# Two-model kernel on one core: the spread of the joined weights of dilated attention issued later, and stick-breaking blocks placed on both halves of the array

## The chip, the cores and the metric

The kernel runs on one core of a Trainium2 chip. The metric is the time of one execution in microseconds of device time; lower is better. Matrix products run on TensorE (PE), loads of its weights are listed apart (PEld), and the other engines are VectorE (DVE), ScalarE (ACT), GpSimd (POOL, which also issues some transfers) and SyncE (SP, which issues the others). PE's sums go to banks of PSUM, everything else lies in SBUF with 128 partitions.

## The reference, cut to what matters

The program computes two models one after the other. The first (a mixer with a recurrent and a state-space branch, and a mixture of experts) is not touched. The second has two layers over 512 tokens of width 1024. Each layer normalises, projects once, runs three attentions over that projection, gates and merges them, and ends in a feed-forward part:

```
h = _rms_norm(x, attn_norm[l])
proj = h @ w_in[l]
...
o_a = _dilated_mixture(aq, ak, a_v.reshape(grp)).reshape(B, S, DSA_OUT)
...
o_c = _stick_breaking_attention(c_q.reshape(sb), c_k.reshape(sb), c_v.reshape(sb)).reshape(B, S, SB_OUT)
gates = jax.nn.sigmoid(gate.reshape(B, S, N_BRANCH, D_MODEL))
```

Stick breaking has 8 heads of width 64. For a block of 128 queries:

```
z = jnp.einsum('bqhd,bkhd->bhqk', qi, k, preferred_element_type=jnp.float32) * scale
strict = kpos[None, :] < qpos[:, None]
log_beta = jax.nn.log_sigmoid(z)
log_one_minus = jnp.where(strict, jax.nn.log_sigmoid(-z), 0.0)
after = lax.cumsum(log_one_minus, axis=3, reverse=True) - log_one_minus
weights = jnp.exp(jnp.where(strict, log_beta + after, -jnp.inf))
return jnp.einsum('bhqk,bkhd->bqhd', weights.astype(v.dtype), v)
```

Dilated attention has 4 heads in each of 3 groups (dilations 1, 4, 16); each group gives an output and the logarithm of its softmax sum per token and head, and the groups are joined by a softmax over those logarithms:

```
wts = jax.nn.softmax(jnp.stack(lses, axis=0), axis=0)
o = jnp.sum(wts[..., None] * jnp.stack(outs, axis=0).astype(jnp.float32), axis=0)
```

## The kernel before

Everything is built in float32. A large product is made of three products of rounded halves (`mm3`: lines 202, 205 and 206), and one 128-row tile of the gates takes 8 times 3 such products of 512 columns. These tiles depend on nothing in the attentions, so the kernel uses them as dense filler: `GATES = (9, 3, 2, 10)` says how many go beside each stage. A small attention product in plain float32 shows as two records (two passes) in the trace.

Two or more generators are woven by `merge`: each yields numbers, its clock advances by that number over the weight it was given, and the generator with the least clock goes next. `mark`, `paced`, `pin` and `after` tie a product to the one issued before it, so that the order of the woven generators stays the order of issue on PE; a scheduler orders the rest by data.

The **stick-breaking stage** of a layer weaves `sb_heads` with 9 gate tiles and half of the query preparation of another attention (`mla_half`). A pass of `sb_heads` issues the logits of head h (`sb_logits`: four diagonal blocks, L385, and three rectangles, L390, of k times q into the three PSUM tiles `z`), then finishes head h-1 (`sb_out`: masks and suffix sums by matrix products, L419 and after, three exponentials into `wt`, and the product with v, L439 and after, which the trace lists partly under L419). Head h uses the 64 partitions from 64*(h%2), so its logits fill 64 of the array's 128 rows; the product with v fills 64 of its 128 columns. The result goes by a DVE copy to `gev` and by a transfer to `od` in memory.

The **dilated stage** weaves `dsa_att` (weight 29.2) with the last 10 gate tiles (240 dense products) and with `branches`, which fetches the other attentions' results. `dsa_att` has 8 units, 4 query blocks for each of two pairs of heads: `logits` (L719 to L725), `softmax` on DVE and ACT, `pv` (transposes L754, products L765). After a pair's fourth unit `both(pr)` transposes the collected maxima and sums (L776), works out the joined weights `T`, two rows of 512 tokens (ACT L779, L781, L782, L785; DVE L780, L783, L784, L786, L787, reciprocal L788, L789), and spreads them over the 128 partitions by two products with the constant `sel` (L793, two rows deep), which L795 and L796 multiply into the outputs. Then `merge2` starts, with its own weights to convert (L183 on ACT, L184 on DVE).

Of the kernel before, what the change touches and what calls it, by code (L numbers as in the profile page):

```python
# [9 lines left out]
F32 = mybir.dt.float32  # L10
# [7 lines left out]
P = 128  # L18
D = 1024
S = 512  # L20
# [216 lines left out]
class Block2(Ctx):  # L237
# [130 lines left out]
    def sb_heads(self, p, pp, qT, kT, v, spill):  # L368
        st = {}
        for h in range(9):  # L370
            if h < 8:
                yield from self.sb_logits(p, pp, h, qT, kT, st)
            if h:
                yield from self.sb_out(p, pp, h - 1, v, st, spill)

    def sb_logits(self, p, pp, h, qT, kT, st):
# [7 lines left out]
        for b in range(4):  # L384
            i = nc.tensor.matmul(at(b * P, (b + 1) * P), k[:, diag(b)], q[:, diag(b)], start=(b == 0), stop=True,  # L385
                                 skip_group_check=True)
        self.mark(i)
        yield 1
        for b in (0, 2, 1):
            i = nc.tensor.matmul(at(*off[b]), k[:, diag(b)], q[:, (b + 1) * P:], start=(b != 2), stop=True,  # L390
                                 skip_group_check=True)
        self.mark(i)
        yield 2
        e = p.tile([P, W], F32, name="e", bufs=2)
# [17 lines left out]
    def sb_out(self, p, pp, h, v, st, spill):  # L412
# [4 lines left out]
        r = slice(64 * (h % 2), 64 * (h % 2) + 64)  # L417
# [21 lines left out]
        nc.tensor.matmul(ob[r, :P], vh[:, 0], wt[:, diag(0)], start=True, stop=False, skip_group_check=True)  # L439
        for b in range(4):  # L440
            if b:
                i = add(ob[r, diag(b)], vh[:, b], wt[:, diag(b)], b == 3)
            if b < 3:
                i = add(ob[r, (b + 1) * P:], vh[:, b], wt[:, slice(*off[b])])
            if b == 1:
                self.mark(i)
                yield 2
        self.mark(i)
        yield 1
        spill(h // 2, ob, r)  # L450
# [251 lines left out]
    def dsa_att(self, p, pp, oa):  # L702
# [69 lines left out]
        def both(pr):  # L772
# [17 lines left out]
            yield 0.5  # L790
            for o in range(2):
                R = pp.tile([P, 512], F32, name=f"s{o}", bufs=2)
                i = nc.tensor.matmul(R, self.k["sel"][:2], T[:, o], start=True, stop=True)  # L793
                self.mark(i)
                nc.vector.tensor_mul((oa[:, pr], oAB[pr][:, 1])[o], oAB[pr][:, o], R)  # L795
            nc.gpsimd.tensor_add(oa[:, pr], oa[:, pr], oAB[pr][:, 1])  # L796
            yield 1.7
# [3 lines left out]
        yield 1.3  # L801
        for n, u in enumerate(units):
# [5 lines left out]
            yield from pv(*u, es, w0)  # L808
            if u[1] == NT - 1:
                yield from both(u[0])  # L810
# [4 lines left out]
    def attn2(self, l, x, hh, hl):  # L815
# [5 lines left out]
        with ExitStack() as es0:  # L821
# [4 lines left out]
            def spill(i, ps, r=slice(0, P)):  # L826
                s = stage.tile([P, S], F32, name="gev", bufs=3)
                nc.vector.tensor_copy(s[r], ps[r])
                nc.gpsimd.dma_start(od[i, r], s[r])

# [17 lines left out]
            with self.pool(f"sb{l}") as p, self.pool(f"sbp{l}", psum=True) as pp:  # L848
# [8 lines left out]
                merge([(self.sb_heads(p, pp, qT, kT, v, spill), 8 * 11.5), (*fill(gates(g0)), -self.KICK2),  # L857
# [1784 lines left out]
```

## Time and profile before

| | |
|---|---|
| median of 3 runs | 4501.78 us (4495.5 to 4502.18) |
| profiled execution | 4502.9 us, span 4501.1 us |
| PE busy | 4108.9 us, 91% of the span |
| DVE, ACT, POOL busy | 2274.7 (51%), 1580.0 (35%), 981.2 us (22%) |
| the first layer's stick-breaking stage | 2471 to about 2630 us |
| the first layer's dilated stage | 2857 to about 2978 us |
| the second layer's | 3519 to about 3678 us, 3902 to about 4023 us |

The span is from the first to the last recorded event; the rest of the profiled execution's time, 1.8 us, lies around it. The granted clock of PE is given as a share of full speed: 1.00 is 2.4 GHz, 0.50 is 1.2 GHz. A busy engine is not one at its peak, and idle time of an engine that nobody waits for costs nothing; what counts is what PE waits for in the two stages.

### The profile page before, as it was taken

What the parts mean: (1) busy time and instruction counts of PE and PEld (TensorE: products, weight loads), DVE (VectorE), ACT (ScalarE), POOL (GpSimd) and SP (SyncE); (2) the same over time, 40 slices, a digit from 0 to 9 for tenths busy, and PEclk for the clock granted to TensorE, in tenths of its full rate; (3) what the DMA queues carried; (4) which work ended last, traced back from release to release, by engine and by line L of the source; (5) the groups of instructions that cost most, each with busy time, mean ns of one, the idle gap of its engine ahead of it and who ended that gap; (6) DMA issues with size and microseconds to landing.
All of it is one profiled execution on the core that took longest, in us unless ns stands there. A gap on an engine that the chain in (4) does not pass through costs nothing. (4 is left out here: it accounts for less than half of the span.)

```text
span 4501.1 us, 70132 instructions
## 1 busy us (share of the span) xinstructions
PE 4108.9 (91%) x28191; PEld 3030.7 (67%) x28191; DVE 2274.7 (51%) x4106; ACT 1580.0 (35%) x3184; POOL 981.2 (22%) x1272
## 2 busy tenths in 40 slices
PE   7899888798898888799998999989999999989998
PEld 5777665576665556444436778768888777858887
DVE  4666766656859865411113255454343244555332
ACT  3333332233346553200003554433233464433331
POOL 1333432334535542200001121130001021211000
PEclk9999999898999999899999999999999999989999
DMA  4222224322342336599993222243332222324332
GB/s 164 68 54 68 66 52 136 82 56 70 110 138 92 110 104 199 214 377 393 394 400 121 62 64 87 78 140 87 98 100 85 73 62 80 94 88 123 96 97 75
DMA packets 535698, 569.04 MB, mean 126 GB/s; under 512 B 126256, under 2 KB 426804, under 8 KB 534348
## 3 DMA queue, kind: packets, MB, share of 16 engines
q1 hardware_dynamic: 400940, 463.04, 30.7%
q0 software_dynamic: 21216, 71.42, 4.8%
q10 hardware_dynamic: 113216, 30.09, 3.2%
q8 instruction: 222, 3.64, 0.3%
q14 instruction: 104, 0.85, 0.1%
HBM read 508.40 MB, written 56.05 MB: 125 GB/s over the span
## 5 line engine op out<-in xcount | busy, mean ns | idle before, releaser
L202 PE MATMUL d<-hh,wh 128*128 128x512 f32 (+1 forms) x1952 | 861.3, 442 | 3.0 <-ACT wh L183 2.0
L205 PE MATMUL d<-hl,wh 128*128 128x512 f32 (+1 forms) x1952 | 782.9, 401 | 14.2 <-DVE hl L184 8.9
L206 PE MATMUL d<-hh,wl 128*128 128x512 f32 (+1 forms) x1952 | 781.1, 400 | 3.7 <-DVE wl L184 3.5
L183 ACT CAST wh<-wr 128x1024 fp32r<-128x1024 f32 (+2 forms) x509 | 433.4, 855 | 925.5 <-PE d L205 427.4
L184 DVE TENSOR_TENSOR wl<-wr,wh 128x1024 fp32r<-128x1024 f32 (+1 forms) x378 | 433.9, 1152 | 627.4 <-ACT wh L183 621.7
L202 PEld LDWEIGHTS d<-hh,wh 128*128 128x128 f32 x1952 | 378.4, 194 | 113.7 <-issue 46.7
L205 PEld LDWEIGHTS d<-hl,wh 128*128 128x128 f32 x1952 | 379.9, 195 | 91.3 <-issue 20.7
L206 PEld LDWEIGHTS d<-hh,wl 128*128 128x128 f32 x1952 | 377.4, 193 | 94.8 <-DVE wl L184 7.5
L184 POOL TENSOR_TENSOR wl<-wr,wh 128x512 fp32r<-128x512 f32 (+1 forms) x131 | 186.7, 1428 | 146.1 <-ACT wh L183 144.9
L202 PE MATMUL d<-wh,hh 128*128 128x256 f32 x704 | 205.4, 292 | 4.4 <-ACT wh L183 3.8
L202 PE MATMUL m<-wh,gh 128*128 128x512 f32 x512 | 200.3, 392 | 7.8 <-ACT wh L183 7.8
L205 PE MATMUL d<-wl,hh 128*128 128x256 f32 x704 | 202.9, 288 | 3.0 <-DVE wl L184 1.7
L206 PE MATMUL d<-wh,hl 128*128 128x256 f32 x704 | 202.0, 287 | 0.0
L205 PE MATMUL m<-wl,gh 128*128 128x512 f32 x512 | 200.3, 391 | 0.0
L206 PE MATMUL m<-wh,gl 128*128 128x512 f32 x512 | 200.0, 391 | 0.0
L202 PEld LDWEIGHTS d<-wh,hh 128*128 128x128 f32 x704 | 136.9, 195 | 6.4 <-ACT wh L183 4.2
L2498 PE MATMUL pa<-ew,XE 128*64 128x512 f32 x496 | 140.7, 602 | 0.0
L1681 POOL TENSOR_SCALAR Sl<-Sall,lam 128x64 f32<-128x64 f32 x176 | 96.1, 559 | 199.7 <-DVE Sall L1693 198.7
L205 PEld LDWEIGHTS d<-wl,hh 128*128 128x128 f32 x704 | 136.8, 194 | 3.9 <-DVE wl L184 2.1
L206 PEld LDWEIGHTS d<-wh,hl 128*128 128x128 f32 x704 | 136.7, 194 | 0.1
L2498 PE MATMUL pb<-ew,XE 128*64 128x512 f32 x504 | 127.9, 597 | 6.2 <-DMA ew<-in_exp_w_dram 6.2
L2498 PE MATMUL py<-ew,ec 128*64 128x512 f32 x512 | 130.5, 598 | 2.3 <-DMA ew<-in_exp_w_dram 2.3
(745 smaller groups left out, 8221.7 us busy)
## 6 DMA issues: line engine op xcount, KB each, us to landing
ew<-in_exp_w_dram SPq DMA_DIRECT2D x189, 1024.0 KB
wr<-in_w_ff_dram SPq DMA_DIRECT2D x128, 512.0 KB
wr<-in_w_in_dram SPq DMA_DIRECT2D x116, 512.0 KB
wr<-in_w_in_dram SPq DMA_DIRECT2D x167, 256.0 KB
wr<-in_ada_w_dram SPq DMA_DIRECT2D x64, 256.0 KB
sg<-gev POOLq DMA_DIRECT2D x48, 256.0 KB, 2.6
sgt<-sg POOLq DMA_DIRECT2D x48, 256.0 KB, 3.2
su<-u POOLq DMA_DIRECT2D x24, 384.0 KB, 3.1
```

The source lines that it names most:

```text
L183: i = self.high(hi, src)
L184: j = self.low.tensor_sub(lo, src, hi.bitcast(F32))
L202: i = nc.tensor.matmul(out, lh, rh, start=start, stop=False)
L205: nc.tensor.matmul(out, lh, rl, start=False, stop=False)
L206: self.latest = nc.tensor.matmul(out, ll, rh, start=False, stop=stop)
L1681: nc.gpsimd.tensor_scalar(Sl[:, d], S[:, d, n], lam[:, d, c:c + 1], None, op0=OP.mult)
L2498: nc.tensor.matmul(ps[c][64 * j:64 * j + 64], lhs(k + i, j), w_, start=(k + i == 0), stop=(k + i == KC - 1))
```

## The change

In the stick-breaking stage, `other(i)` copies the q and k of head pair i into `qk`, with the two groups of 64 partitions exchanged, by four transfers issued on POOL (16 in a layer). `sb_logits` takes the diagonal blocks and the rectangle `off[1]` from the head's own 64 partitions, and the rectangles `off[0]` and `off[2]` from the exchanged copy, in another order and with other yields. The product with v is cut into nine parts that alternate between output partitions 0 to 63 and 64 to 127, and write 256 columns instead of 512; `spill_sb` copies 128x256 instead of 64x512 and stores it with two transfers instead of one. `e` has one buffer instead of two.

In the dilated stage, `both` ends when `T` is computed. Its spread is a function `join`, called for the first pair after the next unit's `pv`, and for the second pair after a further yield of 9; its products are pinned behind the latest dense product. The stage's weight rises from 29.2 to 39, by which fewer dense products fall to each yield before that.

```diff
@@ -366,14 +366,25 @@
     SBO = {0: (512, 896), 2: (896, 1024), 1: (1024, 1280)}
 
     def sb_heads(self, p, pp, qT, kT, v, spill):
-        st = {}
+        st, swap = {}, []
+
+        def other(i):
+
+            x = p.tile([P, 2, S], F32, name="qk", bufs=2)
+            for j, src in enumerate((qT, kT)):
+                self.nc.gpsimd.dma_start(x[:64, j], src[64:, i])
+                self.nc.gpsimd.dma_start(x[64:, j], src[:64, i])
+            swap.append(x)
+        other(0)
         for h in range(9):
+            if h % 2 == 0 and h < 6:
+                other(h // 2 + 1)
             if h < 8:
-                yield from self.sb_logits(p, pp, h, qT, kT, st)
+                yield from self.sb_logits(p, pp, h, qT, kT, swap[h // 2], st)
             if h:
                 yield from self.sb_out(p, pp, h - 1, v, st, spill)
 
-    def sb_logits(self, p, pp, h, qT, kT, st):
+    def sb_logits(self, p, pp, h, qT, kT, qk, st):
         nc = self.nc
         off, W = self.SBO, self.SBW
         diag = lambda b: slice(b * P, (b + 1) * P)
@@ -381,17 +392,21 @@
         q, k = qT[r, h // 2], kT[r, h // 2]
         z = [pp.tile([P, 512], F32, name="z", bufs=6) for _ in range(3)]
         at = lambda a, b: z[a // 512][:, a % 512:a % 512 + b - a]
-        for b in range(4):
-            i = nc.tensor.matmul(at(b * P, (b + 1) * P), k[:, diag(b)], q[:, diag(b)], start=(b == 0), stop=True,
-                                 skip_group_check=True)
+        ro = slice(64 - 64 * (h % 2), 128 - 64 * (h % 2))
+        qo, ko = qk[ro, 0], qk[ro, 1]
+
+        mm = lambda a, b, k, q, start: nc.tensor.matmul(at(a, b), k, q, start=start, stop=True, skip_group_check=True)
+        mm(0, P, k[:, diag(0)], q[:, diag(0)], True)
+        mm(*off[0], ko[:, diag(0)], qo[:, P:], True)
+        for b in (1, 2, 3):
+            i = mm(b * P, (b + 1) * P, k[:, diag(b)], q[:, diag(b)], False)
+        i = mm(*off[2], ko[:, diag(2)], qo[:, 3 * P:], False)
+        self.mark(i)
+        yield 2
+        i = mm(*off[1], k[:, diag(1)], q[:, 2 * P:], True)
         self.mark(i)
         yield 1
-        for b in (0, 2, 1):
-            i = nc.tensor.matmul(at(*off[b]), k[:, diag(b)], q[:, (b + 1) * P:], start=(b != 2), stop=True,
-                                 skip_group_check=True)
-        self.mark(i)
-        yield 2
-        e = p.tile([P, W], F32, name="e", bufs=2)
+        e = p.tile([P, W], F32, name="e")
         pieces = ((0, 512), (512, 1024), (1024, 1280))
         for a, b in pieces:
             nc.scalar.activation(e[:, a:b], at(a, b), AF.Abs)
@@ -414,7 +429,6 @@
         off, W = self.SBO, self.SBW
         diag = lambda b: slice(b * P, (b + 1) * P)
         z, sp, ac = st.pop(h)
-        r = slice(64 * (h % 2), 64 * (h % 2) + 64)
 
         add = lambda o, a, b, stop=False: nc.tensor.matmul(o, a, b, start=False, stop=stop, skip_group_check=True)
         wt = p.tile([P, W], F32, name="wt", bufs=1)
@@ -436,18 +450,19 @@
         yield 1.5
         ob = z[0]
         vh = v[:, :, h * 64:(h + 1) * 64]
-        nc.tensor.matmul(ob[r, :P], vh[:, 0], wt[:, diag(0)], start=True, stop=False, skip_group_check=True)
-        for b in range(4):
-            if b:
-                i = add(ob[r, diag(b)], vh[:, b], wt[:, diag(b)], b == 3)
-            if b < 3:
-                i = add(ob[r, (b + 1) * P:], vh[:, b], wt[:, slice(*off[b])])
-            if b == 1:
+
+        U, D_ = slice(0, 64), slice(64, 128)
+        parts = [(U, 0, 0, 0), (D_, 0, 1, P), (U, P, 3, 3 * P), (D_, P, 2, 2 * P), (U, P, 0, 6 * P), (D_, 0, 0, 4 * P),
+                 (U, P, 2, 7 * P), (U, P, 1, 9 * P), (D_, P, 1, 8 * P)]
+        for n, (x, o, b, c) in enumerate(parts):
+            m = 2 * P if c == 4 * P else P
+            i = nc.tensor.matmul(ob[x, o:o + m], vh[:, b], wt[:, c:c + m], start=(n < 2), stop=True, skip_group_check=True)
+            if n == 3:
                 self.mark(i)
                 yield 2
         self.mark(i)
         yield 1
-        spill(h // 2, ob, r)
+        spill(h, ob)
 
 
     def attend(self, p, pp, units, logits, scale):
@@ -787,18 +802,21 @@
             nc.vector.tensor_add(T[:, 2], T[:, 2], T[:, 3])
             nc.vector.reciprocal(T[:, 2], T[:, 2])
             nc.vector.tensor_mul(T[:, :2], T[:, :2], T[:, 2:3].to_broadcast([2, 2, S]))
-            yield 0.5
+            return T
+
+        def join(pr, T):
             for o in range(2):
                 R = pp.tile([P, 512], F32, name=f"s{o}", bufs=2)
                 i = nc.tensor.matmul(R, self.k["sel"][:2], T[:, o], start=True, stop=True)
+                self.pin(i)
                 self.mark(i)
                 nc.vector.tensor_mul((oa[:, pr], oAB[pr][:, 1])[o], oAB[pr][:, o], R)
             nc.gpsimd.tensor_add(oa[:, pr], oa[:, pr], oAB[pr][:, 1])
-            yield 1.7
 
         units = list(product(range(2), range(NT)))
         nxt = logits(*units[0])
         yield 1.3
+        T = None
         for n, u in enumerate(units):
             w0 = nxt[1]
             es = softmax(*u, *nxt)
@@ -806,8 +824,16 @@
                 nxt = logits(*units[n + 1])
                 yield 1.3
             yield from pv(*u, es, w0)
+            if T is not None:
+                join(u[0] - 1, T)
+                T = None
+                yield 1.7
             if u[1] == NT - 1:
-                yield from both(u[0])
+                T = both(u[0])
+                yield 0.5
+        yield 9
+        join(1, T)
+        yield 1.7
 
 
     GATES = (9, 3, 2, 10)
@@ -827,6 +853,14 @@
                 s = stage.tile([P, S], F32, name="gev", bufs=3)
                 nc.vector.tensor_copy(s[r], ps[r])
                 nc.gpsimd.dma_start(od[i, r], s[r])
+
+            def spill_sb(h, ps):
+                s = stage.tile([P, S], F32, name="gev", bufs=3)[:, :2 * P]
+                nc.vector.tensor_copy(s, ps[:, :2 * P])
+                to = od[h // 2, 64 * (h % 2):64 * (h % 2) + 64].rearrange("p (q t) -> p q t", t=P)
+                v = s.rearrange("p (q t) -> p q t", t=P)
+                nc.gpsimd.dma_start(to[:, ::3], v[:64])
+                nc.gpsimd.dma_start(to[:, 1:3], v[64:])
 
             def gev(i, ps):
                 g = stage.tile([P, S], F32, name="gev", bufs=3)
@@ -854,7 +888,7 @@
                 run(self.tr_gen(w, C2["ck"], 512, hh, hl, KC, lambda i, ps: nc.scalar.copy(kT[:, i], ps)))
                 self.mla_prep1(l, pm)
                 run(self.nat_gen(w, C2["cv"], 512, hh, hl, KC, lambda t, c, m, ps: nc.scalar.copy(v[:, t, c:c + m], ps)))
-                merge([(self.sb_heads(p, pp, qT, kT, v, spill), 8 * 11.5), (*fill(gates(g0)), -self.KICK2),
+                merge([(self.sb_heads(p, pp, qT, kT, v, spill_sb), 8 * 11.5), (*fill(gates(g0)), -self.KICK2),
                        (self.mla_half(l, pm, 0), 18, 0.5)])
                 self.last = None
             pv = es.enter_context(self.pool(f"dsa{l}"))
@@ -876,7 +910,7 @@
                     self.dsa_pad = fill(gates(g2))[0]
                     run(self.dsa_qk(l, pq, px, pp, w, hh, hl))
                 with self.pool(f"dsb{l}") as p:
-                    merge([(self.dsa_att(p, pp, oa), 29.2),
+                    merge([(self.dsa_att(p, pp, oa), 39),
                            (*fill(gates(g3)), -self.KICK2), (self.branches(po, od, sp), 8)])
                     self.last = None
             es.close()
```

The order of issue on PE shows the second join of a layer. `T` are the joined weights, `s0` and `s1` the PSUM tiles that receive the spread, the rows L202, L205 and L206 are dense gate products. Before:

```order
L776 MATMUL t_26182<-ident_65,st_25434 98x128 x4
L202 MATMUL d_26144<-hh_21374,wh2_26140 128x512
L205 MATMUL d_26144<-hl_21375,wh2_26140 128x512
L206 MATMUL d_26144<-hh_21374,wl2_26141 128x512
L793 MATMUL s0_26202<-T_26187,sel_19207 128x512
L793 MATMUL s1_26205<-T_26187,sel_19207 128x512
L202 MATMUL d_26144<-hh_21374,wh2_26140 128x512
```

Of the change, with the first and the last of the dense products between:

```order
L791 MATMUL t_26141<-ident_65,st_25478 98x128 x4
L202 MATMUL d_26134<-hh_21374,wh0_26130 128x512
L205 MATMUL d_26134<-hl_21375,wh0_26130 128x512
...
L205 MATMUL d_26223<-hl_21375,wh2_26219 128x512
L206 MATMUL d_26223<-hh_21374,wl2_26220 128x512
L810 MATMUL s0_26246<-T_26146,sel_19207 128x512
L810 MATMUL s1_26249<-T_26146,sel_19207 128x512
```

Between the transposes and the spread there stood 3 dense products, and now 60. On DVE, the steps of the same `T` (L795 to L804) now have steps of other work between them; `wl` are the low halves of the weights of the stage that follows:

```order
L799 TENSOR_TENSOR T<-t,T 2x512
L801 TENSOR_TENSOR T<-T 2x1024
L802 TENSOR_TENSOR T<-T 2x512
L184 TENSOR_TENSOR wl_26287<-wr_26284,wh_26286 128x1024
L803 RECIPROCAL T<-T 2x512
L184 TENSOR_TENSOR wl_26293<-wr_26290,wh_26292 128x1024
L804 TENSOR_TENSOR T<-T 2x1024
```

Before, no other work stood between the steps of that `T`. The first join on PE, of the change (`pr` are softmax numerators, `pt` their transposes):

```order
L769 MATMUL t_25882<-ident_65,pr1_25837 128x128 x3
...
L780 MATMUL t_25891<-pt1_25886,v2_23243 64x128
L202 MATMUL d_25859<-hh_21374,wh0_25855 128x512
L205 MATMUL d_25859<-hl_21375,wh0_25855 128x512
L206 MATMUL d_25859<-hh_21374,wl0_25856 128x512
L769 MATMUL t_25969<-ident_65,pr0_25935 128x128 x4
L769 MATMUL t_25976<-ident_65,pr1_25941 128x128 x4
L810 MATMUL s0_25903<-T_25811,sel_19207 128x512
L810 MATMUL s1_25906<-T_25811,sel_19207 128x512
```

Before, the first spread came right behind the six products L765 of the unit that follows the pair; now 3 dense products and the 8 transposes of the unit after that stand ahead of it too. The logits of a head, on PE, before (`z` are the three logit tiles):

```order
L385 MATMUL z_22726<-qT_21771,kT_21772 128x128 x4
L202 MATMUL d_22719<-hh_21374,wh2_22715 128x512
L205 MATMUL d_22719<-hl_21375,wh2_22715 128x512
L206 MATMUL d_22719<-hh_21374,wl2_22716 128x512
L390 MATMUL z_22727<-qT_21771,kT_21772 128x384
L390 MATMUL z_22727<-qT_21771,kT_21772 128x128
L390 MATMUL z_22728<-qT_21771,kT_21772 128x256
```

and of the change:

```order
L398 MATMUL z_22758<-qT_21771,kT_21772 128x128
L398 MATMUL z_22759<-qk_22458 128x384
L398 MATMUL z_22758<-qT_21771,kT_21772 128x128 x3
L398 MATMUL z_22759<-qk_22458 128x128
...
L398 MATMUL z_22760<-qT_21771,kT_21772 128x256
```

The rectangles of 384 and 128 columns now stand among the diagonal blocks and read `qk`; six dense products stand ahead of the last rectangle.

## Rows read from the trace of the kernel before

**Rows 1.** Windows: length, busy us of PE, PEld, DVE, ACT, POOL, granted clock, DMA share, GB/s.

```profile
2471.00:2630.00 159.00, 158.37 (x820) 115.84 (x819) 56.22 (x78) 95.61 (x137) 33.41 (x51) 1.00 0.22 64
2857.00:2973.00 116.00, 95.34 (x536) 67.47 (x535) 49.41 (x79) 42.96 (x106) 6.15 (x10) 0.88 0.21 64
```

**Rows 2.** Waits of PE, dilated stage, first layer: total us, times, longest.

```profile
PE s L793 <- DVE T L789: 17.3, 2, 11.2
```

**Rows 3.** Timeline of PE, first join: start, us, what, count, idle before it.

```profile
2899.20 0.60 PE L776 MATMUL t<-ident,st 128*98 128x128 f32 x4
...
2914.10 3.78 PE L793 MATMUL s<-T,sel 2*128 2x512 f32 x4 [6.09 <-DVE T L789]
```

**Rows 4.** Timeline of PE, second join.

```profile
2956.73 0.49 PE L776 MATMUL t<-ident,st 128*98 128x128 f32 x3
...
2969.12 3.78 PE L793 MATMUL s<-T,sel 2*128 2x512 f32 x4 [11.20 <-DVE T L789]
```

**Rows 5.** Windows around the two joins, and their stretches at the lower clock.

```profile
2900.81:2923.10 22.29, 12.83 (x36) 6.98 (x35) 11.58 (x13) 6.15 (x15) 1.81 (x2) 0.63 0.11 36
2957.52:2978.11 20.59, 9.39 (x18) 5.31 (x17) 11.51 (x12) 5.71 (x8) 3.38 (x5) 0.59 0.08 26
2906.50:2923.57 17.07, 10.98 (x28) 6.25 (x28) 7.95 (x7) 1.13 (x2) 1.27 (x1) 0.50 0.00 0
2961.11:2978.18 17.07, 9.06 (x17) 5.37 (x18) 9.83 (x10) 3.30 (x5) 3.38 (x5) 0.50 0.10 31
```

**Rows 6.** Timeline of PE, stick breaking, one head's small products and their ends.

```profile
2530.38 0.43 PE L439 MATMUL z<-wt,v 128*64 128x128 f32 x2
...
2532.04 0.50 PE L202 MATMUL d<-hh,wh 128*128 128x512 f32 x1
...
2532.93 0.87 PE L419 MATMUL z<-wt,v 128*64 128x128 f32 x6
2533.73 0.50 PE L202 MATMUL d<-hh,wh 128*128 128x512 f32 x1
...
2534.62 1.16 PE L385 MATMUL z<-qT,kT 64*128 64x128 f32 x8
2535.70 0.50 PE L202 MATMUL d<-hh,wh 128*128 128x512 f32 x1
...
2536.60 1.56 PE L390 MATMUL z<-qT,kT 64*128 64x384 f32 x6
2538.09 0.50 PE L202 MATMUL d<-hh,wh 128*128 128x512 f32 x1
```

**Rows 7.** Timeline of PE, dilated stage: logits and products with v of one unit.

```profile
2870.91 0.70 PE L721 MATMUL s<-kT,qT 64*128 64x256 f32 x4
...
2871.99 0.51 PE L202 MATMUL d<-hh,wh 128*128 128x512 f32 x1
...
2877.22 1.20 PE L765 MATMUL t<-pt,v 128*64 128x128 f32 x16
```

**Rows 8.** Timeline of POOL and ACT ahead of the stick-breaking stage.

```profile
2475.88 1.00 POOL L601 COPY kn<-kr 128x128 f32<-128x128 f32 x4 [44.33 <-DVE qlTl L197]
...
2455.59 0.58 ACT L854 COPY kT<-d 128x512 f32<-128x512 f32 x1
```

**Rows 9.** Transfers by line, whole run: count, KB each, median us to landing.

```profile
od<-gev POOLq DMA_DIRECT2D x16, 128.0 KB, 2.3
```

**Rows 10.** Timeline of PE, dilated stage: dense products after one unit's logits.

```profile
2881.46 0.50 PE L202 MATMUL d<-hh,wh 128*128 128x512 f32 x1
...
2884.35 0.60 PE L754 MATMUL t<-ident,pr 128*128 128x128 f32 x4
```

**Rows 11.** Groups of DVE instructions, dilated stage: count, busy us, mean ns, idle before.

```profile
L184 DVE TENSOR_TENSOR wl<-wr,wh 128x1024 fp32r<-128x1024 f32 x9 | 11.0, 1222 | 5.4 <-ACT wh L183 5.4
```

**Rows 12.** Timelines of DVE and ACT: first and last step of one unit's softmax.

```profile
2881.56 1.29 DVE L738 TENSOR_REDUCE st<-s 128x2 f32<-128x512 f32 x2 [2.42 <-PE s L725]
...
2887.10 0.48 ACT L744 ACTIVATE pr<-s,sm 128x256 f32<-128x256 f32 x1
```

## Prediction, made before the changed kernel was timed

> **What bounds the kernel now.** I read the windows of the two stages first. In the stick-breaking stage PE is busy 158.4 of 159.0 us at full clock [rows 1]: nothing is waited for, and what counts is how long PE's own products take. In the dilated stage it is busy 95.3 of 116 us at a mean clock of 0.88 [rows 1], so there is idle time and slow time. The waits name the cause: the spread `sel` waits for `T` twice, 17.3 us in total and 11.2 at the longest [rows 2]. The timeline shows both places [rows 3, 4]: PE runs out of work that stands ahead of the spread, and sits idle 6.1 us before the first and 11.2 before the second. The windows around the two show that the harm outlasts the idling: from inside the first, 17.07 us run at clock 0.50 (1.2 GHz), and likewise at the second, and the last of those lie behind the spread [rows 5].
>
> What the two joins cost is window length less what the same products take at full clock. The prices: 12 dense products with their entry fill 2.89 us between logits and transposes [rows 10], of which about 0.11 is the change of array shape, so 0.232 each; a pass of 128 columns takes about 0.107 (14 such block passes in 1.66 us against 6 in 0.80 [rows 6]), so a 512-column pass 0.43. First join: 13 dense 3.0, 6 transposes 0.65, 12 passes of the product with v on both halves 0.65 plus entry 0.25, 4 passes of the spread 1.7, shape changes 0.2: 6.5 of 22.3 us [rows 5], 15.8 lost. Second: 13 dense 3.0, spread 1.7, changes 0.2: 4.9 of 20.6 [rows 5], 15.7 lost. The second layer has the same two waits of the same length, so 63 us are lost at four joins. No more than this can be won in the dilated stage.
>
> **The change part by part.**
>
> *The second join.* 60 dense products instead of 3 stand between the transposes and the spread: 13.9 us, with the transposes 14.4 us of work. The chain of `T` took 12.4 us from transposes to spread (2956.73 to 2969.12 [rows 4]). It gets longer: two subtractions `wl` of the next stage now stand between its steps on DVE, 1.22 us each [rows 11], so about 14.8 us, and PE waits some 0.5 us. That is too short for me to expect a fall of the clock. Saved: about 15 of 15.7 us; 13 if `T` comes 2.5 us late, 15.5 if the subtractions fit in gaps in which DVE waits for ACT. What is late next is L813 and with it `merge2`; the oa halves were waiting there before too, and the gate products of that tile run behind the spread as before.
>
> *The first join.* The chain took 14.9 us here (2899.20 to 2914.10 [rows 3]), longer because the softmax of the next units stands between its steps; I take 15.2, since now the reductions of one more unit do. By the order of issue, ahead of the spread now stand 21 dense products (4.9 us), the logits of a unit (1.6, of which 1.08 are small products [rows 7]), 14 transposes (1.4 us with 0.1 for changes of shape), 12 passes of products with v (0.9) and some 0.4 us of other changes of shape: 9.2 us. So PE still waits about 6 us, as it did before (6.09), only in one place instead of three, and the clock falls afterwards as before; I put 2.3 us on that, between nothing and 4 us (the spread took 3.78 us instead of 1.7 [rows 3], and the dense products behind it ran at half clock until 2923.57 [rows 5]). Lost 8.3 instead of 15.8: saved 7.5, between 2 (chain longer by 3 us, full cost of the clock) and 11 (the chain as before, no fall).
>
> *The dense products that pay for it* are the same 240. Before the spread of pair 1 the stage has about 57 fewer, so each unit has less between its logits and its transposes. Softmax of a unit takes from 2881.56 to 2887.58, 6.0 us, with other work between its steps [rows 12]. Its cover was 12.4 us (logits of one unit end at 2871.99 [rows 7], the transposes of that unit start at 2884.35 [rows 10]). By the order of issue a middle unit keeps 27 dense products (6.3), transposes (0.9), products with v (1.1) and the next logits (1.6): 9.9 us. 6.0 is hidden with nearly 4 to spare: cost 0. If that cover is gone, see the slower rival.
>
> *Stick breaking.* A head's logits took 1.08 and 1.49 us, its product with v 1.66 and 0.80 [rows 6]: 5.03. Do two halves of the array work at once? In the dilated stage they do, in this same kernel: the logits there, 8 block passes on each half, took 1.08 us (2870.91 to 2871.99 [rows 7]), as long as 8 on one half alone (2534.62 to 2535.70 [rows 6]), and 16 passes with v took 1.20 us [rows 7], where one half would take 1.9. So now: logits first part, 8 block passes a half, 1.13; the rectangle alone, 4 passes, 0.66 with entry; product with v, 4 and 6 passes a half, 0.69 and 0.91 with an offset of one pass between halves. Sum 3.39 us; 1.64 saved a head, 26 us for 16 heads. I take 25, because the first two and the last head's products are woven otherwise. The stage is bound by PE, so all of it should show.
>
> How strictly products follow each other is open: in the rows cited, neighbours on the two halves are equally long; here a 384-column rectangle stands among 128-column blocks. The Trainium skill (TensorE: Matmul & The Clock Gate, Part 3, The mechanism) says that products start and end in program order. By that the blocks behind the rectangle wait for its end, and the saving would be smaller; the rival below prices it.
>
> The 16 exchange transfers per layer stand on POOL's queue, which is idle for 44 us up to 2475.88 [rows 8], and the first pair's k is ready at 2456.2 [rows 8], 15 us before the first logits. Like transfers landed in 2.3 us [rows 9]. Later pairs are asked for a head or two ahead, some 15 us. Cost 0; without that cover, about 3 us once a layer. The smaller DVE copy and the second store cost POOL 0.55 us a head where it is busy 33 of 159 us [rows 1]: 0. One buffer of `e` makes a head's first ACT step wait for the previous head's DVE reading of `e`, which is over before that head's sums reach PE: 0. ACT, busy 96 us [rows 1], would then stand against about 146: still not the bound. The head finished last has no other head to hide its chain; 0 to 5 us a layer there is my bound for that, and 0 to 1 what I expect.
>
> **Sum.** 25 + 2 x (7.5 + 15) = 70 us. Against the profiled execution's own 4502.9 us that gives 4432.9; it lies 1.1 us above the median of the runs shown, so 4432 us.
>
> **Rivals.**
> 1. *Ends in order.* If products on both halves end in program order, the first part of a head's logits takes 1.63 us (the rectangle's second pass holds up the next block, and the blocks the last rectangle) and the second group with v 1.13: 0.95 saved a head, 15 us in all, 4442. For it: no row shows unequal neighbours side by side. Against: the full overlap at [rows 7]. Chance 0.13; the page named above states this rule.
> 2. *No overlap within a head.* Operands in `qk` or the alternation of output halves could serialise: nothing saved in stick breaking, 4457. Against: [rows 7]. 0.05.
> 3. *The first join keeps its loss*: `T` later by as much as the spread is moved, since the softmax of another unit stands among its steps. 15 us less: 4447. For it: its steps were already interrupted there; 0.12.
> 4. *The second join still waits.* `T` late by another 5 us because ACT converts the next weights first: PE waits 5.5 us and the clock falls, 9 to 10 us lost at each: 4452. For it: those subtractions in the order; against: no ACT step stands between the last four of `T`. 0.08.
> 5. *Slower: the units starve.* If a unit's softmax took longer than its 9.9 us of cover, each of 16 units would idle, and the clock would halve in much of the stage. At 14 us of softmax, 4 us idle and about 4 of slow time each: 128 us, less the 70 won, 4561. It decides from about 12 us on, where 2.2 us idle and as much slow time cost each unit 4.4. Against: 6.0 at [rows 12]. 0.04, a quarter of that near no change.
>
> That the change doesn't do what it says is excluded by the order of issue for its places, not for its time.
>
> **How the numbers follow.** My forecast has what is left, 0.58, with its own range 4424 to 4447 (upwards the first join at 2 instead of 7.5 or the end of the stage at 5 in both layers and half of the other losses, downwards all three terms at their best: 22 and 31 and 26). Rivals 1 to 4 add 4442 to 4457; 4410 to 4458 leaves out the slower case and some of the unfavourable ends of two at once, about 0.15. What a measurement of this kernel can tell from no change is about 0.2%, 9 us. Faster: 0.96 (forecast and rivals 1 to 4); within: 0.01; slower: 0.03.
>
> **What would show it.** The `sel` products of the second pair wait under 1 us and run at full clock; the first pair's wait about 6 us, in one piece. The stretch of stick breaking falls from 159 [rows 1] to about 146 us, with logits groups of 1.1 and 0.7 us and v groups of 0.7 and 0.9. Logits groups of 1.6 would speak for rival 1, of 2 for rival 2. Waits of transposes for `pr` in every unit would be rival 5. The prediction is wrong if the stage of stick breaking gains a wait for ACT or for `qk`, which I have at nothing.

## The result, and the profile after

The changed kernel takes 4426.3 us (median of 4 runs, 4421.7 to 4442.8) against 4499.0 us of the kernel before on the same chip (the three runs above and a fourth): a ratio of 0.9845, with a 95% interval of 0.9818 to 0.9872. That is 73 us saved, with 58 to 82 us inside the interval; 70 were forecast. The profiled execution has a span of 4426.3 us, 74.8 less than before.

The windows of the four stages after the change: length, busy us of PE, PEld, DVE, ACT, POOL, granted clock, DMA share, GB/s. The first two reach from the first logits of stick breaking to the first transposes of the next attention, the others from the first logits of dilated attention to the first product of the merge.

```profile
2470.88:2623.51 152.63, 151.16 (x914) 115.47 (x914) 56.30 (x85) 100.43 (x149) 44.04 (x72) 1.00 0.28 80
3478.34:3631.79 153.45, 151.48 (x914) 115.49 (x914) 56.28 (x85) 100.45 (x149) 45.08 (x72) 1.00 0.28 80
2837.91:2935.96 98.05, 94.24 (x541) 67.42 (x540) 49.15 (x79) 41.98 (x107) 6.78 (x11) 0.97 0.25 76
3850.08:3948.96 98.88, 95.40 (x540) 68.30 (x540) 49.15 (x79) 41.98 (x107) 6.77 (x11) 0.95 0.25 75
```

The same windows of the kernel before:

```profile
2471.93:2639.29 167.36, 166.33 (x881) 123.18 (x881) 59.06 (x85) 100.83 (x149) 34.95 (x56) 1.00 0.23 67
3519.42:3686.50 167.08, 166.22 (x881) 123.19 (x881) 59.16 (x85) 100.82 (x149) 35.93 (x56) 1.00 0.23 67
2857.22:2975.55 118.33, 97.67 (x540) 69.44 (x540) 50.03 (x79) 43.15 (x107) 7.99 (x13) 0.87 0.21 63
3902.06:4020.24 118.18, 97.52 (x540) 69.44 (x540) 50.02 (x79) 43.15 (x107) 7.99 (x13) 0.87 0.21 63
```

Stick breaking got 14.7 and 13.6 us shorter, and there it is PE's busy time that fell, by 15.2 and 14.7; its idle time was 1.0 and 0.9 us before and is 1.5 and 2.0 now. Dilated attention got 20.3 and 19.3 us shorter, and there most of it is idle time: 20.7 us were not busy before, 3.8 and 3.5 are not now. The four stages together give 67.9 of the 74.8 us; the other 6.9 lie outside these windows, and are taken up below.

What answers to [rows 2], the waits of PE in the first layer's dilated stage of the changed kernel (total us, times, longest):

```profile
PE t L769 <- DVE oab L784: 2.8, 1, 2.8
PE t L780 <- ACT pt L772: 0.6, 1, 0.6
PE s L810 <- DVE T L804: 0.3, 1, 0.3
```

Of 17.3 us of waiting for `T`, 0.3 is left. The second join, which answers to [rows 4] (timeline of PE: start, us, what, count):

```profile
2932.21 0.40 PE L206 MATMUL d<-hh,wl 128*128 128x512 f32 x1
2932.56 1.98 PE L810 MATMUL s<-T,sel 2*128 2x512 f32 x4
```

No wait, and the spread takes 1.98 us instead of 3.78. DVE's last step of `T` there:

```profile
2931.31 1.20 DVE L804 TENSOR_TENSOR T<-T 2x1024 f32<-2x1024 f32 x1
```

It ended at 2932.51, 0.05 us ahead of the spread. The cover is just as long as the chain. The first join, which answers to [rows 3], on PE:

```profile
2874.83 0.60 PE L791 MATMUL t<-ident,st 128*98 128x128 f32 x4
...
2887.97 0.63 PE L769 MATMUL t<-ident,pr 128*128 128x128 f32 x4 [2.81 <-DVE oab L784]
2888.93 3.68 PE L810 MATMUL s<-T,sel 2*128 2x512 f32 x4 [0.33 <-DVE T L804]
```

and on DVE (start, us, line, what):

```profile
2884.24 3.34 DVE L803 RECIPROCAL T<-T 2x512 f32<-2x512 f32 x1
2887.51 0.31 DVE L784 COPY oab<-t 128x128 f32<-128x128 f32 x1
2887.67 1.20 DVE L804 TENSOR_TENSOR T<-T 2x1024 f32<-2x1024 f32 x1
```

Here PE waits 2.81 us for a PSUM tile `t`. Its last reader, DVE's copy of `oab`, stands in DVE's queue behind the reciprocal. When the wait is over, `T` is almost ready, so the spread waits 0.33 only. Behind it PE ran 6.85 us at clock 0.50. In the second layer the wait for `t` is the same 2.81 us, `T` isn't waited for, and the stretch at 0.50 is 10.24 us long:

```profile
2889.05:2895.90 6.85, 6.85 (x12) 3.63 (x13) 1.79 (x3) 1.05 (x2) 1.27 (x1) 0.50 0.00 0
3899.40:3909.64 10.24, 9.51 (x19) 5.68 (x20) 4.78 (x7) 2.13 (x3) 1.68 (x2) 0.50 0.00 0
```

When the changed kernel was run again, it was 10.24 us in both layers.

What answers to [rows 6], one head of stick breaking on PE:

```profile
2525.91 0.66 PE L459 MATMUL z<-wt,v 128*64 128x128 f32 x8
2526.50 0.50 PE L202 MATMUL d<-hh,wh 128*128 128x512 f32 x1
...
2527.39 0.87 PE L459 MATMUL z<-wt,v 128*64 128x128 f32 x10
2528.20 0.50 PE L202 MATMUL d<-hh,wh 128*128 128x512 f32 x1
...
2529.08 0.37 PE L398 MATMUL z<-qT,kT 64*128 64x128 f32 x1
2529.09 0.59 PE L398 MATMUL z<-qk 64*128 64x384 f32 x1
2529.30 0.38 PE L398 MATMUL z<-qT,kT 64*128 64x128 f32 x2
2529.51 0.48 PE L398 MATMUL z<-qk 64*128 64x384 f32 x1
...
2530.17 0.50 PE L202 MATMUL d<-hh,wh 128*128 128x512 f32 x1
...
2531.76 0.70 PE L398 MATMUL z<-qT,kT 64*128 64x256 f32 x2
2532.39 0.39 PE L433 MATMUL z<-mk_sb_b,ident_b 128*128 128x512 bf16 x1
```

From start to the start of what follows: product with v 0.59 and 0.81, logits 1.09 and 0.63, 3.12 us where there were 5.03. The middle rows show how: the first rectangle (`qk`, the other half) starts 0.01 us after the first pass of the first diagonal block, and two more passes on the head's own half start at 2529.30 and after it, before the rectangle's second pass at 2529.51. The first block has two passes, so the third one on its half is of the second block; in the order of issue the rectangle, with both its passes, stands ahead of that block.

### The profile page after: what moved, and what is told of

Its sections match the earlier page's. It is cut to its first block, busy times and chain, and to the rows that moved or that the text cites. A ratio compares the mean times of both kernels' runs of the same rounds, so it can differ in the third digit from the quotient of the medians.

```text
span 4426.3 us, 70343 instructions
## 1 busy us (share of the span) xinstructions
PE 4059.9 (92%) x28255; PEld 2997.1 (68%) x28255; DVE 2266.0 (51%) x4106; ACT 1576.9 (36%) x3184; POOL 1005.9 (23%) x1320
## 5 line engine op out<-in xcount | busy, mean ns | idle before, releaser
L202 PE MATMUL d<-hh,wh 128*128 128x512 f32 (+1 forms) x1952 | 856.3, 439 | 3.7 <-ACT wh L183 2.6
L205 PE MATMUL d<-hl,wh 128*128 128x512 f32 (+1 forms) x1952 | 779.2, 399 | 14.4 <-DVE hl L184 9.2
L206 PE MATMUL d<-hh,wl 128*128 128x512 f32 (+1 forms) x1952 | 778.1, 399 | 5.7 <-DVE wl L184 5.6
L202 PEld LDWEIGHTS d<-hh,wh 128*128 128x128 f32 x1952 | 377.0, 193 | 106.3 <-issue 38.8
L206 PEld LDWEIGHTS d<-hh,wl 128*128 128x128 f32 x1952 | 375.2, 192 | 96.2 <-DVE wl L184 9.6
L205 PEld LDWEIGHTS d<-hl,wh 128*128 128x128 f32 x1952 | 377.3, 193 | 91.6 <-issue 21.3
L202 PE MATMUL d<-wh,hh 128*128 128x256 f32 x704 | 204.5, 291 | 6.2 <-ACT wh L183 5.7
L202 PE MATMUL m<-wh,gh 128*128 128x512 f32 x512 | 200.0, 391 | 7.9 <-ACT wh L183 7.9
L205 PE MATMUL d<-wl,hh 128*128 128x256 f32 x704 | 202.2, 287 | 3.1 <-DVE wl L184 1.7
L206 PE MATMUL d<-wh,hl 128*128 128x256 f32 x704 | 201.4, 286 | 0.0
L205 PE MATMUL m<-wl,gh 128*128 128x512 f32 x512 | 200.1, 391 | 0.0
L206 PE MATMUL m<-wh,gl 128*128 128x512 f32 x512 | 199.7, 390 | 0.0
L202 PEld LDWEIGHTS d<-wh,hh 128*128 128x128 f32 x704 | 136.3, 194 | 8.2 <-ACT wh L183 6.1
L205 PEld LDWEIGHTS d<-wl,hh 128*128 128x128 f32 x704 | 136.3, 194 | 3.9 <-DVE wl L184 2.1
L206 PEld LDWEIGHTS d<-wh,hl 128*128 128x128 f32 x704 | 136.2, 193 | 0.1
```

Of the source, the lines that this page charges most:

```text
L202: i = nc.tensor.matmul(out, lh, rh, start=start, stop=False)
L205: nc.tensor.matmul(out, lh, rl, start=False, stop=False)
L206: self.latest = nc.tensor.matmul(out, ll, rh, start=False, stop=stop)
```

## The experiments

Two stages are told apart in every profile by their lengths, taken as in the windows above from the starts of the same PE products (us, first layer / second layer):

| kernel | ratio to before (95%) | stick breaking | dilated |
|---|---|---|---|
| before | 1 | 167.4 / 167.1 | 118.3 / 118.2 |
| changed | 0.9845 (0.9818 to 0.9872) | 152.6 / 153.5 | 98.1 / 98.9 |
| changed, again | 0.9842 (0.9825 to 0.9860) | 152.7 / 153.4 | 98.6 / 98.8 |
| stick-breaking part alone | 0.9934 (0.9919 to 0.9949) | 152.6 / 153.5 | 118.5 / 118.0 |
| dilated part alone | 0.9899 (0.9884 to 0.9914) | 167.4 / 167.1 | 98.9 / 98.8 |
| blocks first | 0.9855 (0.9839 to 0.9872) | 155.8 / 155.8 | 98.0 / 98.8 |
| copy on ACT | 0.9849 (0.9825 to 0.9874) | 152.7 / 153.4 | 97.7 / 98.3 |
| no hold | 0.9909 (0.9894 to 0.9924) | 152.7 / 153.4 | 113.5 / 113.5 |
| old weight | 0.9887 (0.9868 to 0.9905) | 152.6 / 153.4 | 104.0 / 104.0 |
| first join later | 0.9820 (0.9806 to 0.9835) | 152.7 / 153.5 | 93.8 / 94.4 |
| the same, again | 0.9811 (0.9795 to 0.9827) | 152.7 / 153.5 | 93.7 / 94.7 |
| the same, logits in one group | 0.9833 (0.9818 to 0.9847) | 151.8 / 151.8 | 94.4 / 92.1 |

The stages repeat within 1 us from kernel to kernel where nothing in them is changed, apart from the last line's dilated stage in the second layer, which is taken up there. What is outside them doesn't repeat: the first logits of the changed kernel start at 2470.88 us in one profile and at 2482.66 in the other. So the stages tell of an effect of a few us that the ratios can't.

**The stick-breaking part alone.** The kernel before, with the parts of the change that concern `sb_heads`, `sb_logits`, `sb_out` and `spill_sb`:

```diff
-                merge([(self.sb_heads(p, pp, qT, kT, v, spill), 8 * 11.5), (*fill(gates(g0)), -self.KICK2),
+                merge([(self.sb_heads(p, pp, qT, kT, v, spill_sb), 8 * 11.5), (*fill(gates(g0)), -self.KICK2),
```

> The kernel before with the change of the stick-breaking stage alone (exchanged copies, blocks on both halves, the new split of the product with v, the new store). If the two parts of the change are independent: the two stick-breaking stages give 28 us of the 73 that the whole change gave (first logits to the first product of the attention after it: 167.4 to 152.6 and 167.1 to 153.5 us in the profiles), so about 4471 us, and the waits for T before the spread are 17.3 us a layer as before. If the change in the dilated stage had helped the other (earlier arrival of weights), the time falls by less than 20 us.

4477.0 us, 27.5 below the 4504.6 us of the kernel before in that group. The stick-breaking stages are those of the changed kernel to 0.1 us, the dilated ones those of before, and `T` is waited for 17.6 us in the first layer.

**The dilated part alone.** The kernel before, with `both`, `join`, the loop over the units and the weight of the changed kernel:

```diff
-                    merge([(self.dsa_att(p, pp, oa), 29.2),
+                    merge([(self.dsa_att(p, pp, oa), 39),
```

> The kernel before with the change of the dilated stage alone (join called later, yield of 9, weight 39). If independent: the dilated stages give 40 us (118.3 to 98.1 and 118.2 to 98.9 us from the first logits to the first product of the merge), so about 4459 us, with the second spread unwaited and one wait of 2.8 us for DVE's copy of oab before the first. If the two parts need each other, the sum of this gain and that of the stick-breaking change alone is under 60 us.

4459.9 us, 44.7 below. With the other part that makes 72.2 us, the whole change. Neither needs the other.

**Blocks first.** The changed kernel with another order inside the first group of logits:

```diff
-        mm(0, P, k[:, diag(0)], q[:, diag(0)], True)
+        for b in range(4):
+            i = mm(b * P, (b + 1) * P, k[:, diag(b)], q[:, diag(b)], b == 0)
         mm(*off[0], ko[:, diag(0)], qo[:, P:], True)
-        for b in (1, 2, 3):
-            i = mm(b * P, (b + 1) * P, k[:, diag(b)], q[:, diag(b)], False)
```

> The changed kernel, with the four diagonal blocks of a head issued first and the two rectangles of the other half behind them, nothing else. Theory A, each half of the array takes its own products as they come, looking past products of the other half that stand ahead in the program: the first part of a head's logits stays near 1.09 us and the time within 3 us of the changed kernel's. Rival, products start in program order and only neighbours run side by side: the first part takes nearly the sum of both halves, 1.6 to 1.9 us, 0.5 to 0.8 us more for each of 16 heads, 8 to 13 us slower than the changed kernel. Between them: PE looks a few products ahead, so that the last of the four blocks overlap with the rectangles, 1.4 to 1.6 us.

The time lies between the two, as the third case says. The group's 1.61 us lies on the border of that case and the rival, so the rows have to decide. One head's group on PE:

```profile
2529.54 0.82 PE L398 MATMUL z<-qT,kT 64*128 64x128 f32 x5
2530.09 0.59 PE L398 MATMUL z<-qk 64*128 64x384 f32 x1
2530.20 0.49 PE L398 MATMUL z<-qT,kT 64*128 64x128 f32 x3
2530.52 0.70 PE L398 MATMUL z<-qk 64*128 64x384 f32 x3
2531.15 0.50 PE L202 MATMUL d<-hh,wh 128*128 128x512 f32 x1
```

The group took 1.61 us instead of 1.09. The first pass on the other half starts when three passes of the own half are still to start, no earlier; in 14 of the 16 heads it starts 0.55 us behind the group's first, as here. So PE does take products of the other half past ones that stand ahead of them, but only a few passes far. The stages got 3.2 and 2.4 us longer, 5.6 together, less than 16 times 0.52. So the alternating order of the change is worth about 6 us of its 28.

**First join later.** The changed kernel, with the first spread behind the second unit of the second pair:

```diff
-            if T is not None:
+            if T is not None and u[1] == 1:
```

> The changed kernel, with the first pair's spread called one unit later (after the second unit of the second pair instead of after the first). The first join of the changed kernel still waits 2.8 us for DVE's copy of oab, which stands behind the reciprocal, and then runs 6.8 us at clock 0.50: some 6.5 us a layer. If this loss is from too little work of other units between T and its spread: both go, no stretch at 0.50 around the spread, and the time falls by 12 to 13 us, to about 4413 us. Rival: the wait only moves to the next step of the units that needs DVE behind the reciprocal (the copy pt or oab), then 2 us at most are won.

The wait behind the reciprocal is gone, and none of its size took its place: PE waits 0.5 and 0.6 us for `pt` in the whole stage of the first layer. But only 4.3 and 4.5 us a layer were won, not the expected 6.5: the clock fell behind the first spread all the same, and one wait of 0.5 us for `pt` is new. It fell once more behind the second spread, mostly after the end of the stage (2931.86). PE at the first spread and the two stretches at clock 0.50 of the first layer:

```profile
2894.15 1.98 PE L810 MATMUL s<-T,sel 2*128 2x512 f32 x4
2896.06 0.50 PE L202 MATMUL d<-hh,wh 128*128 128x512 f32 x1
```

```profile
2897.35:2900.75 3.40, 3.40 (x11) 1.77 (x11) 0.88 (x1) 1.54 (x2) 0.98 (x2) 0.50 0.00 0
2931.47:2934.88 3.41, 3.41 (x10) 2.63 (x9) 1.99 (x3) 2.14 (x4) 3.01 (x5) 0.50 0.29 88
```

Each begins 1.3 us behind the end of a spread, at 2896.06 and 2930.21, with PE busy throughout and dense products on both sides; each costs half of 3.4 us. The last wait ahead of them, 0.5 and 0.6 us for `pt`, ended at 2891.54 and 2911.23. The second layer shows the same two stretches, and so do both layers when it was run again. With 4422.9 us here and 4419.0 when run again (5 runs) this version has the lowest medians measured, 85 us below the 4504.3 of before. The expectation for running it again:

> The kernel with the first join one unit later once more, with more rounds. The profiles of the first time show the dilated stage 4.3 and 4.5 us shorter than the changed kernel's, so 8 to 10 us below the changed kernel: ratio to the kernel before about 0.982 to 0.9825. If those differences between runs were chance, the ratio is that of the changed kernel, 0.984 to 0.9845.

0.9811 is in line with the first of its two cases; its interval ends at 0.9827 and overlaps with those of the changed kernel, which begin at 0.9818 and 0.9825, so the ratios alone say little, and the stages (93.7 and 94.7 us) say it.

**The changed kernel again**, so that the next ones stand beside it:

> The changed kernel once more, unaltered, so that the others of this group are compared with it on the same chip. Expected within 6 us of the 73 us gain that was measured.

4430.3 against 4502.1 us, 71.8 less.

**Copy on ACT.** The changed kernel, with the copy that held up the transposes taken off DVE:

```diff
-            nc.vector.tensor_copy(self.by4(oAB[pr][:, 1])[:, qt], op[:, 1])
+            (nc.scalar.copy if (pr, qt) == (1, 0) else nc.vector.tensor_copy)(self.by4(oAB[pr][:, 1])[:, qt], op[:, 1])
```

> The changed kernel, with one copy of oab (the unit after the first pair) on ACT instead of DVE, where it stood behind the reciprocal and where the transposes ahead of the first spread waited 2.8 us for it. Theory: the cause of the first join's loss is the length of the chain of T on DVE (14.1 us) against the work ahead of its spread; the copy only decided which product waits. Then the wait moves from the transposes to the spread itself, 2.5 to 3.5 us for T, and the time stays within 3 us. Rival: the copy was the cause; then the wait is gone and 5 us a layer, 10 us in all, are won.

The wait moved on, though not to `T`: products with v now wait for the other piece of work that stands behind the reciprocal, the copy `pt`. The waits of PE:

```profile
PE t L780 <- DVE pt L772: 1.9, 1, 1.9
PE t L780 <- ACT pt L772: 0.6, 1, 0.6
PE t L769 <- ACT pr L759: 0.4, 1, 0.4
```

The wait was expected at the spread, for `T`; there it didn't come. The stages are 0.4 and 0.6 us shorter than in the first profile of the changed kernel. It is the reciprocal with too little work of PE beside it, not that one copy.

**No hold.** The changed kernel without the last yield:

```diff
-        yield 9
         join(1, T)
```

> The changed kernel without its last yield of 9, so that the second spread comes 3 dense products after its transposes, with the weight of 39 and the late first join kept. If the 57 dense products held back are what hides the second chain of T: PE waits 11 us again at each second spread and runs behind it at clock 0.50, 15 us a layer lost, some 30 us slower than the changed kernel (about 4456 us), and nothing else changes. Rival: part of the gain there comes from calling the join outside of both, then less than 20 us are lost.

31 us above the changed kernel (4461.3 against 4430.3 in the same group), 15.5 and 14.6 us in the stages. The second spread, on PE:

```profile
2930.49 3.78 PE L810 MATMUL s<-T,sel 2*128 2x512 f32 x4 [11.21 <-DVE T L804]
```

It is that of [rows 4] again, to 0.01 us. The 57 products that were held back are the whole gain at the second join.

**Old weight.** The changed kernel, with the old weight for the stage:

```diff
-                    merge([(self.dsa_att(p, pp, oa), 39),
+                    merge([(self.dsa_att(p, pp, oa), 29.2),
```

> The changed kernel with the old weight of 29.2 for the dilated stage: the yield of 9 and the late first join are kept, but the dense products are not held back, so that 9 of them are left between the second pair's transposes and its spread instead of 60, and 39 instead of 21 stand ahead of the first. If the cover by dense products is all that matters: the second spread waits some 9 to 10 us with slow time behind it, 13 to 15 us a layer lost against the changed kernel, while the first join wins 3 to 6 us a layer: 15 to 24 us slower than the changed kernel, about 4445 to 4452 us. Rival: the place of the call is what matters and dense products come from elsewhere in the weave, then under 5 us are lost.

4451.2 us, a ratio of 0.9887 against 0.9845 and 0.9842, so 19 to 20 us slower: cover is what matters. The second spread waits as said:

```profile
2956.15 3.78 PE L810 MATMUL s<-T,sel 2*128 2x512 f32 x4 [10.08 <-DVE T L804]
```

The stages show 6.0 and 5.1 us of it, since the first join got cheaper: 1.3 us of waiting for the copy of `oab` instead of 2.8. Another 3.2 and 5.2 us at clock 0.50 lie behind the end of the stages, where no gate product is left behind the spread; half of that, 4.2 us, is lost. That makes 15 us; where the other 4 to 5 lie isn't shown.

**Logits in one group.** The version with the later first join, and the last rectangle directly behind the other blocks:

```diff
-        self.mark(i)
-        yield 2
         i = mm(*off[1], k[:, diag(1)], q[:, 2 * P:], True)
         self.mark(i)
-        yield 1
+        yield 3
```

> The kernel with the first join one unit later (4422.9 us before), and in stick breaking the last rectangle issued right behind the other blocks, in one group, with the yields of both at its end. A change of array shape costs about 0.2 us in and out together; one group of 6 blocks on one half and 4 on the other should take 1.5 us instead of 1.08 and 0.63. Expected 0.2 us a head, 2 to 3 us in all, if PE stays the bound; 0 or a loss if the logits come too early for the three tiles z, or too late for ACT.

The stages of stick breaking are 0.9 and 1.7 us shorter, 2.6 in all, as expected. The ratio, 0.9833, doesn't show it; that of the version without it is 0.9811 and 0.9820. No better version can be claimed from it. Its dilated stages, unchanged in the program, differ by 2.4 us: the mean granted clock is 0.97 in the first layer's and 1.00 in the second's, where no stretch at 0.50 follows either spread.

## Why the prediction was right

*The sum* was 70 us, and 73 were measured (71.8 when run again). Its terms, against the stages:

| term | forecast | measured |
|---|---|---|
| stick breaking, both layers | 25 | 28.4 (14.7 + 13.6) |
| dilated attention, both layers | 45 | 39.6 (20.3 + 19.3) |
| elsewhere | 0 | 6.9 in these two profiles |

That the sum came within 3 us is partly luck: stick breaking gave 3.4 us more than forecast, the dilated stages 5.4 less, and what closes the gap lies outside the stages.

*Stick breaking* was under-sized. A head went from 5.03 to 3.12 us, 1.9 saved, where 1.64 was worked out. The two v groups were counted 0.10 us too long each (0.69 and 0.91 forecast, 0.59 and 0.81 measured), about the offset of one pass that I allowed between the two halves; in the logits both halves start within 0.01 us. Sixteen times 1.9 would be 31; PE's busy time fell by 29.9 in the two stages, since the first heads are woven with other products, and its idle time rose by 1.6. The second layer's waits:

```profile
PE d L202 <- ACT v L615: 0.7, 1, 0.7
PE z L433 <- DVE sp L419: 0.5, 1, 0.5
PE z L459 <- ACT wt L449: 0.4, 1, 0.4
PE t L636 <- ACT qT L639: 0.2, 1, 0.2
```

I had put a gained wait for ACT or for `qk` as a sign of being wrong. There is none for `qk`; those for ACT went from 0.9 to 1.3 us in the first layer and from 0.7 to 1.3 in the second, too little to touch the sum.

*Rival 1*, products that end in program order, is refuted by the rows of the changed kernel: passes of the second block start before the rectangle's second pass, and the group takes 1.09 us, not 1.63. The rule of the Trainium skill on which it stood (TensorE: Matmul & The Clock Gate, Part 3, The mechanism: products start and end in program order) doesn't hold for these two-pass products on different rows of the array; here the measurement decides. The blocks-first run bounds it: past a few passes the order of the program counts again, and 1.61 us was measured, close to what rival 1 had priced for the change's own order. Rival 2, no overlap, falls by the same rows.

*The second join* went as forecast: 15 us a layer were put on it, and taking the hold away costs 15.5 and 14.6. The late chain of `T` that I put at 0.5 us of waiting ended 0.05 us before it was needed. So rival 4 fell, but with next to no margin.

*The first join* was forecast to keep a wait of 6 us in one piece for `T`. In the first layer it has 2.81 us for a PSUM tile and 0.33 for `T`. Two sizes were off. From transposes to spread the chain took 14.1 us (2874.83 to 2888.93) where I had put 15.2, and the work of PE ahead of the spread 14.1 less 3.1, so 11.0 us, where I had 9.2. The step "PE still waits about 6 us" is the one that failed; the slow time behind it was put at 2.3 us, and half of the busy time at half clock is 3.4 in the first layer and 4.8 in the second, 4.6 and 4.7 when run again. Waiting and slow time together cost 6.6 and 7.6 us, 7.4 and 7.5 when run again, instead of 8.3. A wait put too long and a slow time put too short nearly cancel, so this term came near its forecast by luck. Rival 3, the loss kept whole, falls.

By this the dilated stage should have got shorter by at least the 22.5 us a layer that were forecast, and it got 20.3 and 19.3 shorter. A part of the difference lies behind the end of the stage, where before the clock stayed at 0.50 for another 2.63 and 2.42 us:

```profile
2961.11:2975.55 14.44, 6.43 (x10) 3.32 (x11) 8.11 (x7) 1.24 (x2) 1.84 (x3) 0.50 0.00 0
2975.55:2978.18 2.63, 2.63 (x8) 2.05 (x7) 1.73 (x3) 2.06 (x4) 1.54 (x3) 0.50 0.63 203
4020.24:4022.66 2.42, 2.42 (x7) 1.93 (x6) 1.52 (x3) 2.05 (x4) 1.55 (x3) 0.50 0.66 219
```

Half of it, 1.3 and 1.2 us, was the second join's loss too, and stands under "elsewhere". Inside the first layer's window 20.7 us were idle before, and 17.4 busy us lay in the stretches at half clock (10.98 [rows 5] and 6.43), 8.7 lost: 29.4, with the 1.3 behind the stage 30.7, where 31.5 had been worked out. Inside it now 3.8 us are idle and 3.4 are lost to the clock: 7.2. That is 22.2 less, and the stage is 20.3 shorter. The other 1.9 us (1.7 in the second layer) went into PE's busy time: the same products take that much longer together than at full clock before. PE's timeline changes from one kind of product to another 87 times instead of 84, too few to explain it; it stays open.

*The units* didn't starve (rival 5): the only wait of a unit that doesn't lie at the first join is 0.6 us for `pt`, and none is for `pr`. *The exchange transfers* were hidden: the first logits start at 2470.88 without a wait for `qk`, and nothing else in the stage waits for them.

*Elsewhere*: of the 6.9 us of the profiled difference, 2.5 are the slow time behind the dilated stages. The other 4.4 lie in parts that are the same in both kernels. The first logits started at 2482.66 instead of 2470.88 us when the changed kernel was run again, so such a difference between two profiles is within what one kernel shows.

## What to carry to other kernels

Small products that use half of the array can be doubled up if their operands lie on the other half too; alternate them in the program, since with one half's blocks first the other half started only when three passes of the first were left. A serial chain on slow engines costs PE twice, in idle time and in slow time behind it, and independent dense products held back for it return both; hold back as many as the chain is long, because fewer return little more than their own length (with 9 instead of 3, the wait was 10.1 us instead of 11.2) and the clock still falls. Where one engine's queue holds a long instruction, moving the work behind it one by one only hands the wait on; moving the consumer away from it removed it here.

## What the runs showed that I had not expected

PE's halves run past the order of the program: three passes of the own half were still to start when the other half began (blocks first, 2530.09). And the clock can fall where no wait stands just ahead: in the kernel with the later first join, 3.4 us at 0.50 began 0.1 to 1.5 us behind the end of all eight spreads with `sel`, a product two rows deep, of its two profiles, with PE busy on both sides. With the copy on ACT such a stretch follows the second spread of both layers. The changed kernel has the same spread among the same dense products at its second join, and in neither of its profiles does such a stretch follow there; with the logits in one group it follows both spreads of the first layer and neither of the second. What decides between them was not found out.
